# First head of the expert routing: where its query weights lie, shift products ahead of the query, squares summed on VectorE, and eight choices routed first

## The chip, the cores and the metric

The kernel runs on one core of one Trainium2 chip. The metric is device time in microseconds (us) of one execution; the time before is the median of three runs. The engines are TensorE (PE in the rows; PEld is its weight load), VectorE (DVE), ScalarE (ACT), GpSimd (POOL) and SyncE (SP). SP issues the weight loads in one queue, POOL issues the gathers in its own, and ACT issues a few small loads.

## The reference, cut to what matters

Two transformer blocks on 256 tokens of width 1024. The first block ends with `peer`, a layer of 16,384 tiny experts that the tokens choose by product keys:

```python
qh = (t @ w_q).reshape(T, PEER_HEADS, 2, PEER_KEY_DIM // 2)
s = jnp.einsum('thpd,hpnd->thpn', qh, sub_keys)      # 128 keys in each of 2 halves
s_top, i_top = lax.top_k(s, PEER_TOPK)               # 16 of each half
cand = s_top[:, :, 0, :, None] + s_top[:, :, 1, None, :]
cand_idx = i_top[:, :, 0, :, None] * PEER_N_KEYS + i_top[:, :, 1, None, :]
best, pos = lax.top_k(cand.reshape(T, PEER_HEADS, 256), PEER_TOPK)
idx = jnp.take_along_axis(cand_idx..., pos, axis=-1)
g = jax.nn.softmax(best, axis=-1)
ue, ve = jnp.take(u_tab, idx, axis=0), jnp.take(v_tab, idx, axis=0)
act = jax.nn.gelu(jnp.einsum('thkd,td->thk', ue, t))
return jnp.einsum('thk,thkd->td', g * act, ve)
```

There are 8 heads, and `t` is the normed and shifted input: x times a gain, divided by its root mean square, plus a shift from the modulation. Each token sums 8 times 16 experts, one row of `u_tab` and one of `v_tab` for each.

## The kernel before, in words

The 256 tokens are two tiles of 128. A head and a tile make a step s = 2 * head + tile, so there are 16 steps of 16 choices. For each choice POOL gathers one row of the joined table `uv` (1024 floats of u and 1024 of v) for each of 128 tokens: 256 gathers of 1 MB. They land in a ring of NR = 13 places (tag `uv`). For each, `first` takes the dot product of the u half with the token's row `ht` on VectorE (L943) and the Gelu on ScalarE (L944); `second` makes a diagonal tile `dgw` on VectorE (L952) and multiplies it with the v half in 8 products on TensorE. When `second` is done the place is free and the next gather is issued. The steps of `routing(s + 2)` stand between the dots of step s.

What stands ahead of the first gather: the last products of the previous stage (the `wmix` sum, weights split into high and low parts `whi`, `wlo`, `wlox`), the sum into `x` (L408), then head 0's query (`query_early`). `project` multiplies head 0's query weights `wq` with `xg`, which is x times the gain but not yet normed; so the scores are scaled afterwards by `rs` (from the sums of squares, L351 and L353), and the part that the shift contributes (`pc`, then `pb`: products of the modulation columns with `wq`, and of the result with the keys `ks`) is added. `routing(0)` follows on VectorE: the best 8 of each half (L812, L813), the next 8 (L814 to L816), the 256 sums `cd`, their best 16, and `decode`, which turns positions into row numbers `IX` with one-hot tiles `oh` (L915 to L922). Only then are `normed` and `rows` issued (the normed input `hf`, and its transposed rows `ht`), and gathers go out.

The weights of the eight query heads are loaded by SP in one queue: heads 0 to 3 into four places of the ring, 1 MB each, heads 4 to 7 in halves into places of the earlier weight tiles (`raw`, `whi`, `wlo`). The first nine gathers take ring places that hold no weights, the tenth takes head 0's, and the eleventh to the thirteenth need those of heads 1, 2 and 3, which their projections free. In the program as built, head 0's place is one whose former content was last read by an early product of the `wmix` sum. The place of `ht` lies at bytes 217,888 to 226,080 of each partition, over the last two low parts of `wmix` (bytes 215,808 to 224,000).

Of the kernel before, what the change touches and what calls it, by code (L numbers as in the profile page):

```python
# [113 lines left out]
class Kern:  # L114
# [641 lines left out]
    def phase_b(self):  # L756
# [4 lines left out]
        with ExitStack() as es:  # L761
# [10 lines left out]
            def qload(h):  # L772

                if h < 4:
                    g = rows_.tile([P, 2 * D], F32, name="wq", tag="uv", bufs=NR)
                    self.take(g[:].rearrange("p (u c) -> p u c", u=2), A["wpq"][2 * h:2 * h + 2].rearrange("u p c -> p u c"))
                    wq[h] = [g[:, 0:D], g[:, D:2 * D]]
                else:
                    wq[h] = []
                    for u in (2 * h, 2 * h + 1):  # L780
                        g = self.slot("r", ["raw", "whi", "raw", "whi", "raw", "whi", "wlo", "wlo"][u - 8], F32, "st")
                        self.take(g[:], A["wpq"][u])
                        wq[h].append(g[:])

            self.inturn = True
            for h in range(8):
                qload(h)
# [11 lines left out]
            ht = rows_.tile([P, 2, D], F32, name="ht")  # L799

            def rows():

                for t in range(2):
                    for h in range(2):
                        ps = self.rot("tr")
                        for k in range(4):
                            nc.tensor.transpose(ps[:, k * 128:k * 128 + 128], hf[:, 4 * h + k, t * 128:t * 128 + 128], self.con("ident"))
                        nc.scalar.activation(ht[:, t, h * 512:h * 512 + 512], ps[:], AF.Copy)

            def top16(v, idx, s, n):  # L810
                s2 = wk.tile([P, n], F32, name="s2", tag=f"s2{n}", bufs=1)
                nc.vector.max(v[:, 0:8], s)  # L812
                nc.vector.max_index(idx[:, 0:8], v[:, 0:8], s)  # L813
                nc.vector.match_replace(s2[:], v[:, 0:8], s, -3e38)  # L814
                nc.vector.max(v[:, 8:16], s2[:])
                nc.vector.max_index(idx[:, 8:16], v[:, 8:16], s2[:])  # L816
# [11 lines left out]
            def keys(h, ps):  # L828

                ks = wk.tile([P, 256], F32, name="ks", tag="ks", bufs=2)  # L830
                nc.gpsimd.dma_start(ks[:], A["keysT"][h]) if h < 2 else nc.scalar.dma_start(ks[:], A["keysT"][h])
# [15 lines left out]
            def query_early():  # L847

                ps = project(0, xg)
                sums = self.square_sums(x)  # L850
                rs = self.rms_col(sums)
                sc, ks, end = keys(0, ps)

                pc = self.rot("mm")
                with self.tc.issue_after(end):
                    for a in range(2):
                        for k in range(KT):
                            self.mm(pc[:, a * 128:a * 128 + 128], wq[0][a][:, k * 128:k * 128 + 128],
                                    self.mod[:, 24 + k:25 + k].to_broadcast([P, 128]), k == 0 and a == 0, k == KT - 1 and a == 1)
                cb = wk.tile([P, 256], F32, name="cb", tag="s2256", bufs=1)  # L860
                nc.scalar.activation(cb[:], pc[:, 0:256], AF.Copy)
                pb = self.rot("mm")
                for a in range(2):
                    self.mm(pb[:, a * 128:a * 128 + 128], cb[:, a * 128:a * 128 + 128], ks[:, a * 128:a * 128 + 128])
                for t in range(2):
                    c = slice(t * 256, t * 256 + 256)
                    nc.scalar.activation(scores[0][:, c], sc[:, c], AF.Copy, scale=rs[:, t:t + 1])
                ss = scores[0][:].rearrange("p (t k) -> p t k", t=2)
                nc.vector.tensor_tensor(ss, pb[:, 0:256].unsqueeze(1).to_broadcast([P, 2, 256]), ss, OP.add)
                return rs  # L870

            def normed(rs):
                self.spread(rs, bc[:])
# [5 lines left out]
            IX, WT = {}, {}  # L879

            def routing(s):
# [6 lines left out]

                def half(a):
                    ss = scores[h]  # L890
                    top16(SV[:, a, :], SI[:, a, :], ss[:, t * 256 + a * 128:t * 256 + a * 128 + 128], 128)
# [13 lines left out]
                def decode():  # L905
                    si = wk.tile([P, 2, 16], F32, name="si", tag="si", bufs=1)
                    nc.vector.tensor_scalar(si[:, 0, :], SI[:, 0, :], 128.0, None, op0=OP.mult)
                    nc.vector.tensor_copy(si[:, 1, :], SI[:, 1, :])
                    ab = wk.tile([P, 2, 16], U32, name="ab", tag="ab", bufs=1)
                    nc.vector.tensor_scalar(ab[:, 0, :], BI[:], 4, None, op0=OP.logical_shift_right)  # L910
                    nc.vector.tensor_scalar(ab[:, 1, :], BI[:], 15, None, op0=OP.bitwise_and)
                    af = wk.tile([P, 2, 16], F32, name="af", tag="af", bufs=1)
                    nc.vector.tensor_copy(af[:], ab[:])
                    oh = wk.tile([P, 2, 16, 16], F32, name="oh", tag="oh", bufs=1)
                    nc.vector.tensor_tensor(oh[:].rearrange("p a k c -> p (a k) c"),  # L915
                                            self.con("iota", 16).unsqueeze(1).to_broadcast([P, 32, 16]),
                                            af[:].rearrange("p a k -> p (a k)").unsqueeze(2).to_broadcast([P, 32, 16]), OP.is_equal)
                    nc.vector.tensor_tensor(oh[:], oh[:], si[:].unsqueeze(2).to_broadcast([P, 2, 16, 16]), OP.mult)
                    ix = wk.tile([P, 2, 16], F32, name="ixf", tag="ixf", bufs=1)
                    nc.vector.tensor_reduce(ix[:], oh[:], mybir.AxisListType.X, OP.add)  # L920
                    IX[s] = wk.tile([P, 16], U32, name="IX", tag="IX", bufs=4)
                    last = nc.vector.tensor_tensor(IX[s][:], ix[:, 0, :], ix[:, 1, :], OP.add).ins  # L922
# [5 lines left out]
                return [lambda: half(0), lambda: half(1), pairs, decode]  # L928
# [4 lines left out]
            def fetch(s, k):  # L933
                g = ring[s, k] = rows_.tile([P, 2 * D], F32, name="uv", tag="uv", bufs=NR)
                nc.gpsimd.indirect_dma_start(out=g[:], out_offset=None, in_=A["uv"],  # L935
                                             in_offset=bass.IndirectOffsetOnAxis(ap=IX[s][:, k:k + 1], axis=0))

            def first(s, k):
# [4 lines left out]
                dot = nc.vector.tensor_tensor_reduce(u, u, ht[:, t, :], 1.0, 0.0, OP.mult, OP.add, accum_out=a[:, 0:1]).ins  # L943
# [16 lines left out]
            rs = query_early()  # L960
            for step in routing(0):
                last = step()
            with self.tc.issue_after(last):
                normed(rs)
                rows()
                for step in routing(1):
                    step()
            choices = [(s, k) for s in range(16) for k in range(16)]
# [534 lines left out]
```

## Time and profile before

| what | value |
|---|---|
| three runs | 1529.53, 1532.02, 1536.04 us |
| the profiled execution's own time | 1538.33 us |
| its span | 1536.2 us |
| mean granted TensorE clock | 0.987 |
| busy: PE, PEld, DVE, ACT, POOL | 91%, 83%, 76%, 39%, 23% |
| chain that ended last | PE 49%, DMA 30%, DVE 14%, issue 4% |
| moved by DMA | 433.40 MB, of it 269.24 MB by POOL's gathers |

The profiled execution took 6.3 us more than the median of the three runs. Shares over the whole span mix three parts: a stretch up to about 265 us in which TensorE works through dense products, the gathers from 265 to about 920 us, and the second block from there on. In rows with two numbers in front, the first is the start in us from the span's start and the second the time in us.

### The profile page before, as it was taken

Reading aid. Unit: us, or ns where it says so; the run is one execution under the profiler, and the core shown is the slowest. Engines: PE = TensorE matmul, PEld = TensorE weight load, DVE = VectorE, ACT = ScalarE, POOL = GpSimd, SP = SyncE. Lnnn points to the kernel's source line nnn. Section 1 sums busy time; section 2 is a strip of 40 time slices with the busy share of each in tenths; the row PEclk is TensorE's granted clock in tenths of the full one; section 3 lists DMA queues with packets and bytes.
Section 4 is the critical chain, followed back from the end, with each engine's and each line's share of the span. In section 5 each row is a group of like instructions: output and inputs, shape, how many; then the busy total and the mean of one; then the engine's idle time right before and its main releaser. Section 6 shows DMA issues by size and latency. Waiting matters only on the chain.

```text
span 1536.2 us, 28266 instructions
## 1 busy us (share of the span) xinstructions
PE 1391.3 (91%) x10732; PEld 1275.5 (83%) x10732; DVE 1171.4 (76%) x2760; ACT 603.5 (39%) x1227; POOL 353.0 (23%) x316
## 2 busy tenths in 40 slices
PE   8999986999998787888688889999999999999998
PEld 2898886898987777777677779989999996899997
DVE  4898764897897779776566557976988888588885
ACT  2646532411211113111110004775655568555553
POOL 0000000343465555555455530000000000000000
PEclk9999998999999999999999999999999999999999
DMA  9667745999999999999999994434655542355550
GB/s 349 231 233 264 236 169 212 383 401 421 370 425 426 426 426 426 426 426 426 425 426 426 426 416 163 137 125 151 206 187 185 190 154 97 111 193 188 184 190 28
DMA packets 82839, 433.40 MB, mean 282 GB/s; under 512 B 9296, under 2 KB 10448, under 8 KB 49680
## 3 DMA queue, kind: packets, MB, share of 16 engines
q0 software_dynamic: 37120, 269.24, 42.1%
q1 hardware_dynamic: 43712, 159.67, 30.5%
q10 hardware_dynamic: 1872, 2.68, 0.5%
q8 instruction: 85, 1.39, 0.4%
q14 instruction: 50, 0.41, 0.1%
HBM read 430.51 MB, written 1.05 MB: 281 GB/s over the span
## 4 chain that ended last, share of the span: by engine, by line
PE 49%; DMA 30%; DVE 14%; issue 4%; ACT 1%; POOL 0%; another core or an unknown queue 0%; DVEq 0%; POOLq 0%; SPq 0%; ACTq 0%
PE b L132 48%; DMA uv<-in_uv,IX 27%; DVE uv L943 2%; DMA rawx<-in_wmodT 1%; DVE wlo L209 1%; DVE wlox L209 1%; DVE dgw L952 1%; DVE rawx L488 1%; DMA raw<-in_wmodT 1%; DVE raw L488 1%; DVE s L814 1%; DMA raw<-in_wqkv 1%; DVE SI L816 0%; DVE oh L915 0%; DVE SI L813 0%
## 5 line engine op out<-in xcount | busy, mean ns | idle before, releaser
L132 PE MATMUL b<-dgw,uv 128*128 128x128 f32 x4096 | 506.0, 279 | 99.2 <-DVE dgw L952 98.6
L132 PEld LDWEIGHTS b<-dgw,uv 128*128 128x128 f32 x4096 | 473.0, 192 | 133.4 <-DVE dgw L952 131.8
L943 DVE CUSTOM_DVE_ANT_0 uv<-uv,ht 128x1024 f32<-128x1024 f32 x256 | 312.4, 1220 | 143.6 <-DMA uv<-in_uv,IX 142.0
L935 POOL DMA_INDIRECT uv<-in_uv,IX x256 | 330.3, 1290 | 331.7 <-DMA uv<-in_uv,IX 138.4
L132 PE MATMUL b<-H,whi 128*128 128x256 f32 x1296 | 245.0, 287 | 3.6 <-DVE mx L1041 1.4
L944 ACT ACTIVATE act<-act 128x1 f32<-128x1 f32 x256 | 51.3, 202 | 499.3 <-DVE act L943 489.7
L132 PE MATMUL b<-H,wlox 128*128 128x256 f32 x824 | 231.7, 281 | 0.0
L132 PE MATMUL b<-H,whix 128*128 128x256 f32 x1216 | 221.5, 282 | 0.0
L132 PEld LDWEIGHTS b<-H,whi 128*128 128x128 f32 x1296 | 201.4, 189 | 10.6 <-issue 5.0
L132 PEld LDWEIGHTS b<-H,whix 128*128 128x128 f32 x1216 | 186.7, 188 | 5.3 <-issue 3.0
L132 PEld LDWEIGHTS b<-H,wlox 128*128 128x128 f32 x824 | 155.6, 189 | 0.4 <-issue 0.3
L132 PE MATMUL b<-H,wlo 128*128 128x256 f32 x440 | 122.3, 288 | 0.0
L952 DVE TENSOR_SCALAR dgw<-cn,act,we 128x128 f32<-128x128 f32 x256 | 87.6, 342 | 14.3 <-ACT act L944 14.2
L209 DVE TENSOR_TENSOR wlox<-rawx,whix 128x1024 fp32r<-128x1024 f32 x60 | 73.1, 1222 | 31.7 <-ACT whix L200 30.9
L200 ACT ACTIVATE whix<-rawx 128x1024 fp32r<-128x1024 f32 x60 | 63.0, 1058 | 74.8 <-PE b L132 63.1
L200 ACT ACTIVATE whi<-rawx 128x1024 fp32r<-128x1024 f32 x59 | 62.2, 1058 | 60.1 <-PE b L132 60.1
L209 DVE TENSOR_TENSOR wlox<-raw,whix 128x1024 fp32r<-128x1024 f32 x57 | 69.6, 1221 | 19.0 <-ACT whix L200 18.4
L200 ACT ACTIVATE whi<-raw 128x1024 fp32r<-128x1024 f32 x58 | 61.0, 1056 | 56.9 <-PE b L132 45.8
L132 PEld LDWEIGHTS b<-H,wlo 128*128 128x128 f32 x440 | 82.2, 188 | 1.2 <-issue 0.7
L200 ACT ACTIVATE whix<-raw 128x1024 fp32r<-128x1024 f32 x57 | 60.3, 1058 | 54.0 <-PE b L132 50.8
L353 POOL TENSOR_TENSOR rs<-ms,nhalf 128x2 f32<-128x2 f32 x6 | 6.2, 1027 | 312.9 <-DVE ms L351 312.9
L1256 DVE SCALAR_TENSOR_TENSOR c<-u,cl,c 128x256 f32<-128x256 f32 x176 | 73.7, 478 | 0.8 <-ACT c L1253 0.7
(348 smaller groups left out, 2240.8 us busy)
## 6 DMA issues: line engine op xcount, KB each, us to landing
rawx<-in_wup SPq DMA_DIRECT2D x45, 512.0 KB, 3.3
raw<-in_wup SPq DMA_DIRECT2D x43, 512.0 KB, 3.3
raw<-in_wdn SPq DMA_DIRECT2D x23, 512.0 KB, 3.2
rawx<-in_win SPq DMA_DIRECT2D x21, 512.0 KB, 4.6
rawx<-in_wdn SPq DMA_DIRECT2D x21, 512.0 KB, 3.3
rawx<-in_wmodT SPq DMA_DIRECT2D x18, 512.0 KB, 4.1
raw<-in_wmodT SPq DMA_DIRECT2D x14, 512.0 KB, 3.4
raw<-in_win SPq DMA_DIRECT2D x13, 512.0 KB, 5.1
```

The lines of the kernel that those rows point to most:

```text
L132: return self.nc.tensor.matmul(out, lhsT, rhs, start=start, stop=stop).ins
L200: nc.scalar.activation(hi[:], raw[:], AF.Copy)
L209: nc.vector.tensor_sub(u.lo[:], u.raw[:], u.hi[:].bitcast(F32))
L353: nc.gpsimd.tensor_tensor(rs[:], ms[:], self.nhalf[:, 0:2], OP.pow)
L488: self.nc.vector.tensor_tensor_reduce(r, r, row[h][:], 1.0, self.mod[:, at:at + 1] if h else self.col("bmod", at), OP.mult, OP.add, accum_ ...
L814: nc.vector.match_replace(s2[:], v[:, 0:8], s, -3e38)
L935: nc.gpsimd.indirect_dma_start(out=g[:], out_offset=None, in_=A["uv"], in_offset=bass.IndirectOffsetOnAxis(ap=IX[s][:, k:k + 1], axis=0))
L943: dot = nc.vector.tensor_tensor_reduce(u, u, ht[:, t, :], 1.0, 0.0, OP.mult, OP.add, accum_out=a[:, 0:1]).ins
L944: nc.scalar.activation(a[:, 1:2], a[:, 0:1], AF.Gelu)
L952: done = nc.vector.tensor_scalar(dg[:], self.con("ident"), a[:, 1:2], e[:, k:k + 1], op0=OP.mult, op1=OP.mult).ins
L1256: nc.vector.scalar_tensor_tensor(c[:, a, :], u[:, a, j:j + 256], self.col("cw2", at + 44 * j), c[:, a, :], op0=OP.mult, op1=OP.add)
```

## The change

- Head 0's weights are given the place of `ht` (tag `ht`, one buffer) in place of a ring place; heads 1 and 2 lie in ring places, heads 3 to 6 in places of earlier weight tiles, and head 7 is loaded later, at choice 36, into head 3's places. So seven heads are loaded ahead of the gathers where there were eight, and three projections ahead of the first dot become two (`query` of heads 3 to 7 stands at choices 8, 36, 68, 100, 132, where heads 4 to 7 stood at 8, 36, 68, 100).
- The shift products `pc` stand ahead of `project(0)`; the squares of x are added on VectorE (3 adds of 128x512), which leaves 4 column-sum products where there were 16.
- The scores of head 0 are one operation for each tile on VectorE (scores * rs + shift part), where ScalarE scaled and VectorE added.
- `first8` routes 8 choices from the best 8 of each half (64 sums) into `IX8`; the first 8 gathers use it, and only then do the normed input, the rows and the rest of `routing(0)` follow. Gathers 9 to 13 use `IX`, which holds all 16.
- The prefetch of `wqkv` stands at choice 136 (was 104), and `angles` at 144 (was 120).

SP's queue, where the query weights begin (before with -, after with +; `wq` are whole heads, `raw`, `whi` and `wlo` halves; in brackets the semaphores waited for):

```order
 L181 DMA raw<-in_wmix 128x1024 [waits DMAHW7_49,DVE_49]
-L181 DMA wq<-in_wpq 128x2x1024 [waits PE_49]
-L181 DMA wq<-in_wpq 128x2x1024 [waits DVE_49,DMAHW0_49,PE_49,Activation_49]
-L181 DMA wq<-in_wpq 128x2x1024 [waits DMAHW5_49,DMAHW3_49]
-L181 DMA wq<-in_wpq 128x2x1024 [waits DMAHW4_49]
-L181 DMA raw<-in_wpq 128x1024
+L181 DMA wq<-in_wpq 128x2x1024 [waits DVE_49,PE_49]
+L181 DMA wq<-in_wpq 128x2x1024 [waits DMAHW3_49]
+L181 DMA wq<-in_wpq 128x2x1024 [waits DMAHW4_49,DMAHW0_49,Activation_49]
+L181 DMA raw<-in_wpq 128x1024 [waits DMAHW5_49]
```

The first whole head waited for PE alone, and now waits for PE and DVE: in the program as built, the PE count that it waits for is the one that the last `wmix` product raises, because that product reads the low part which lies where head 0's weights now go. Heads 1 and 2 stand behind it in the same queue.

TensorE, from the last `wmix` product to head 0's scores and the spread of `rs`, before:

```order
L132 MATMUL b_2146<-mh,wlox 128x256
L132 MATMUL b_2623<-cn_69,sq 128x1 x4
L132 MATMUL b_2606<-H_2556,wq 128x256 x16
L132 MATMUL b_2623<-cn_69,sq 128x1 x12
L132 MATMUL b_2656<-ks,qT 128x128 x4
L132 MATMUL b_2662<-mod,wq 128x128 x16
L132 MATMUL b_2681<-ks,cb 128x128 x2
L132 MATMUL b_2734<-dg,cn_69 128x256
```

The same place after:

```order
L132 MATMUL b_2146<-mh,wlox 128x256
L132 MATMUL b_2603<-mod,wq 128x128 x16
L132 MATMUL b_2632<-H_2556,wq 128x256 x16
L132 MATMUL b_2649<-cn_69,sq 128x1 x4
L132 MATMUL b_2660<-ks,cb 128x128 x2
L132 MATMUL b_2665<-ks,qT 128x128 x4
L132 MATMUL b_2676<-dg,cn_69 128x256
```

The shift products (`mod,wq`) moved from behind the scores to the front, and 12 of 16 column sums are gone.

VectorE, from the best 8 of head 0's 64 sums on, after (`cd_2689` holds the sums, `IX_2693` is `IX8`, `t_` are tiles of the normed input):

```order
L820 MAX best<-cd_2689 128x8
L821 MAX_INDEX BI<-best,cd_2689 128x8
L928 TENSOR_SCALAR ab<-BI 128x8
L929 TENSOR_SCALAR ab<-BI 128x8
L931 CAST af<-ab 128x16
L933 TENSOR_TENSOR oh<-cn_69,af 128x128
L936 TENSOR_TENSOR oh<-oh,si 128x128
L938 TENSOR_REDUCE ixf<-oh 128x16
L939 TENSOR_TENSOR IX_2693<-ixf 128x8
L903 TENSOR_TENSOR t_2724<-H_2556,bc_72 128x256
L903 TENSOR_TENSOR t_2727<-H_2556,bc_72 128x256
L827 MATCH_REPLACE s_2773<-SV,ss 128x128
```

The decode of the first eight row numbers, 128 elements wide, follows one round on 64 candidates, and the second rounds (`MATCH_REPLACE`) come behind it; before, two rounds for each half, two on 256 candidates and a decode 512 elements wide stood ahead of any row number.

The diff, cut to its core:

```diff
-                if h < 4:
-                    g = rows_.tile([P, 2 * D], F32, name="wq", tag="uv", bufs=NR)
+                if h < 3:
+                    g = rows_.tile([P, 2 * D], F32, name="wq", tag="uv" if h else "ht", bufs=NR if h else 1)
+                    wq[h] = [g[:, 0:D], g[:, D:2 * D]]
+                    return g
+                wq[h] = [self.slot("r", w, F32, "st") for w in
+                         ("wlo" if h == 6 else "raw", "wlo" if h == 6 else "whi")]
...
+            places = {h: qplace(h) for h in (2, 1, 0)}
             self.inturn = True
-            for h in range(8):
-                qload(h)
+            for h in range(7):
+                if h >= 3:
+                    qplace(h)
+                qload(h, places.get(h))
             self.inturn = False
...
-                ps = project(0, xg)
-                sums = self.square_sums(x)
-                rs = self.rms_col(sums)
-                sc, ks, end = keys(0, ps)
 
                 pc = self.rot("mm")
...
+                sq = [wk.tile([P, 512], F32, name="sq", tag=t, bufs=n) for t, n in [("oh", 1), ("qT", 2), ("qT", 2)]]
+                for b in range(4):
+                    q = sq[b] if b < 2 else sq[2]
+                    nc.scalar.activation(q[:], x[:, 2 * b:2 * b + 2, :].rearrange("p a t -> p (a t)"), AF.Square)
+                    if b:
+                        nc.vector.tensor_tensor(sq[0][:], sq[0][:], q[:], OP.add)
+                with self.tc.issue_after(end):
+                    ps = project(0, xg)
...
+                    nc.vector.scalar_tensor_tensor(scores[0][:, c], sc[:, c], rs[:, t:t + 1], sb[:], op0=OP.mult, op1=OP.add)
                 return rs
...
+                def first8():
+
+                    for a in range(2):
+                        top8(SV[:, a, :], SI[:, a, :], of(a))
+                    cd = wk.tile([P, 64], F32, name="cd8", tag="s2128", bufs=1)
+                    nc.vector.tensor_tensor(cd[:].rearrange("p (a b) -> p a b", a=8),
+                                            SV[:, 0, 0:8].unsqueeze(2).to_broadcast([P, 8, 8]),
+                                            SV[:, 1, 0:8].unsqueeze(1).to_broadcast([P, 8, 8]), OP.add)
+                    top8(best, BI, cd[:])
+                    early.append(wk.tile([P, 8], U32, name="IX8"))
+                    return parts(8, 8, BI[:, 0:8], 3, early[0][:])
...
-            for c in choices[0:NR]:
-                fetch(*c)
-            for h in range(1, 4):
+            choices = [(s, k) for s in range(16) for k in range(16)]
+            query_early()
+            steps = routing(0)
+            last = steps.pop(0)()
+            for c in choices[0:8]:
+                fetch(*c)
+            with self.tc.issue_after(last):
+                normed()
                 rows()
+                for step in steps:
+                    last = step()
+            for c in choices[8:NR]:
+                fetch(*c)
+            with self.tc.issue_after(last):
                 for step in routing(1):
                     step()
...
+            for h in range(1, 3):
                 query(h)
...
-                if n in (8, 36, 68, 100):
-                    query(4 + n // 32)
-                if n == 104:
+                if n in (8, 36, 68, 100, 132):
+                    query(3 + n // 32)
+                if n == 36:
+                    qplace(7)
+                    qload(7)
+                if n == 136:
                     self.allowed = "ac"
                     self.fetch([])
-                if n == 120:
+                if n == 144:
```

## Rows read from the trace of the kernel before

**Rows 1.** The page, DMA rate (GB/s) in 40 equal slices of the span (38.4 us each)

```profile
GB/s 349 231 233 264 236 169 212 383 401 421 370 425 426 426 426 426 426 426 426 425 426 426 426 416 163 137 125 151 206 187 185 190 154 97 111 193 188 184 190 28
```

**Rows 2.** Timeline of POOL: start us, time us, operation, idle before and its releaser

```profile
264.98 1.06 POOL L935 DMA_INDIRECT uv<-in_uv,IX  x1 [16.67 <-DVE SV L812]
...
280.31 0.94 POOL L935 DMA_INDIRECT uv<-in_uv,IX  x1 [2.81 <-PE b L132]
289.38 0.94 POOL L935 DMA_INDIRECT uv<-in_uv,IX  x1 [8.13 <-PE b L132]
297.27 1.61 POOL L935 DMA_INDIRECT uv<-in_uv,IX  x1 [6.95 <-PE b L132]
...
909.02 1.38 POOL L935 DMA_INDIRECT uv<-in_uv,IX  x1 [1.06 <-DMA uv<-in_uv,IX]
```

**Rows 3.** Windows: busy us of each engine, granted clock, DMA share, GB/s

```profile
257.00:265.00 8.00, 0.38 (x1) 0.41 (x2) 7.70 (x34) 0.40 (x2) 0.02 (x1) 0.60 0.00 0
290.00:340.00 50.00, 47.65 (x367) 45.72 (x367) 50.00 (x195) 15.54 (x33) 19.27 (x19) 1.00 0.95 376
...
380.00:420.00 40.00, 39.25 (x316) 38.08 (x315) 32.27 (x85) 9.55 (x26) 18.70 (x16) 1.00 0.98 369
450.00:900.00 450.00, 361.74 (x2883) 333.11 (x2881) 317.64 (x776) 67.17 (x219) 239.00 (x179) 1.00 1.01 426
```

**Rows 4.** Timeline of SP, the queue of the weight loads

```profile
216.79 0.43 SPq L181 DMA_DIRECT2D wq<-in_wpq  x1
...
237.02 2.52 SPq L181 DMA_DIRECT2D wq<-in_wpq  x3
...
242.04 0.33 SPq L181 DMA_DIRECT2D raw<-in_wpq  x1
```

**Rows 5.** Timeline of PE, from the last wmix product to head 0's shift part

```profile
236.66 0.28 PE L132 MATMUL b<-mh,wlox 128*128 128x256 f32 x1
...
236.78 0.95 PE L132 MATMUL b<-cn,sq 128*128 128x1 f32 x8
...
237.59 7.15 PE L132 MATMUL b<-H,wq 128*128 128x256 f32 x32
...
247.18 1.14 PE L132 MATMUL b<-ks,qT 128*128 128x128 f32 x8
...
248.15 5.37 PE L132 MATMUL b<-mod,wq 128*128 128x128 f32 x32
...
253.99 0.71 PE L132 MATMUL b<-ks,cb 128*128 128x128 f32 x4 [0.47 <-ACT cb L861]
```

**Rows 6.** Windows around two falls of the clock (columns as in Rows 3)

```profile
248.00:252.00 4.00, 4.00 (x23) 4.00 (x23) 0.00 (x0) 0.84 (x2) 0.31 (x1) 0.57 1.03 421
...
258.00:260.00 2.00, 0.00 (x0) 0.00 (x0) 1.93 (x10) 0.00 (x0) 0.00 (x0) 0.67 0.00 0
260.00:272.00 12.00, 5.55 (x15) 3.89 (x16) 11.72 (x50) 5.01 (x12) 5.50 (x6) 0.50 0.43 156
```

**Rows 7.** Timeline of DVE and POOL, from the sum into x to the first row numbers

```profile
236.98 0.88 DVE L408 SCALAR_TENSOR_TENSOR x<-b,g1h,x 128x256 f32<-128x256 f32 x2 [0.55 <-PE b L132]
...
247.35 0.16 DVE L351 TENSOR_SCALAR ms<-b 128x2 f32<-128x2 f32 x1 [9.49 <-PE b L132]
247.60 0.72 POOL L353 TENSOR_TENSOR rs<-ms,nhalf 128x2 f32<-128x2 f32 x1 [19.15 <-DVE ms L351]
...
255.53 0.49 DVE L812 MAX8 SV<-ss 128x8 f32<-128x128 f32 x2
...
256.00 0.28 DVE L813 FIND_INDEX8 SI<-SV,ss 128x8 uint32<-128x128 f32 x1
...
258.42 0.40 DVE L895 TENSOR_TENSOR cd<-SV 128x256 f32<-128x256 f32 x1
...
261.74 0.69 DVE L915 TENSOR_TENSOR oh<-cn,af 128x512 f32<-128x512 f32 x1
...
263.91 0.17 DVE L922 TENSOR_TENSOR IX<-ixf 128x16 uint32<-128x16 f32 x1
```

More of the change, by code (lines that the diff above doesn't have):

```diff
@@ L770, in phase_b, with qplace, qload @@
             wq = {}
[L772 to L783 removed]
+            def qplace(h):
+                if h < 3:
[4 more added lines that the diff above has]
+                         ("wlo" if h == 6 else "raw", "wlo" if h == 6 else "whi")]
+            def qload(h, g=None):
+                if g is not None:
+                    self.take(g[:].rearrange("p (u c) -> p u c", u=2), A["wpq"][2 * h:2 * h + 2].rearrange("u p c -> p u c"))
+                    return
+                for u in range(2):
+                    self.take(wq[h][u][:], A["wpq"][2 * h + u])
+            places = {h: qplace(h) for h in (2, 1, 0)}
             self.inturn = True
[L786 to L787 removed]
+            for h in range(7):
+                if h >= 3:
+                    qplace(h)
+                qload(h, places.get(h))
             self.inturn = False
@@ L847, in query_early @@
             def query_early():
-                ps = project(0, xg)
-                sums = self.square_sums(x)
-                rs = self.rms_col(sums)
-                sc, ks, end = keys(0, ps)
                 pc = self.rot("mm")
[L855 to L859, printed above, removed]
+                for a in range(2):
+                    for k in range(KT):
+                        end = self.mm(pc[:, a * 128:a * 128 + 128], wq[0][a][:, k * 128:k * 128 + 128],
+                                      self.mod[:, 24 + k:25 + k].to_broadcast([P, 128]), k == 0 and a == 0, k == KT - 1 and a == 1)
                 cb = wk.tile([P, 256], F32, name="cb", tag="s2256", bufs=1)
                 nc.scalar.activation(cb[:], pc[:, 0:256], AF.Copy)
+                sq = [wk.tile([P, 512], F32, name="sq", tag=t, bufs=n) for t, n in [("oh", 1), ("qT", 2), ("qT", 2)]]
[6 more added lines that the diff above has]
+                    ps = project(0, xg)
+                sums = self.rot("tr")
+                for h in range(2):
+                    for t in range(2):
+                        self.mm(sums[:, t:t + 1], sq[0][:, h * 256 + t * 128:h * 256 + t * 128 + 128], self.con("ones", 1),
+                                h == 0 and t == 0, h == 1 and t == 1)
+                rs = self.rms_col(sums)
+                ks = wk.tile([P, 256], F32, name="ks", tag="ks", bufs=2)
+                nc.gpsimd.dma_start(ks[:], A["keysT"][0])
                 pb = self.rot("mm")
@@ new lines, in first8 @@
+                def first8():
+                    for a in range(2):
+                        top8(SV[:, a, :], SI[:, a, :], of(a))
[6 more added lines that the diff above has]
+                    return parts(8, 8, BI[:, 0:8], 3, early[0][:])
@@ L926, in decode @@
                     return last
-                return [lambda: half(0), lambda: half(1), pairs, decode]
+                return [first8] * (s == 0) + [lambda: half(0), lambda: half(1), pairs, decode]
             big = self.bigs()
@@ L935, in fetch @@
                 nc.gpsimd.indirect_dma_start(out=g[:], out_offset=None, in_=A["uv"],
-                                             in_offset=bass.IndirectOffsetOnAxis(ap=IX[s][:, k:k + 1], axis=0))
+                                             in_offset=bass.IndirectOffsetOnAxis(
+                                                 ap=early[0][:, k:k + 1] if s == 0 and k < 8 else IX[s][:, k:k + 1], axis=0))
             def first(s, k):
```

77 lines of the change are left out of this document (40 added, 37 removed).

## The prediction

> **What bounds the kernel now.** I began with the page's DMA rates by slice [rows 1]: from the twelfth slice to the twenty-third (422 to 883 us) the rate is flat at 425 or 426 GB/s. There the kernel is bound by its transfers, in the middle of a span whose busiest engine is TensorE. Next the queue of POOL [rows 2]: the first gather is issued at 264.98 us and the 256th at 909.02, so 255 pitches take 644.04 us, 2.53 us each. At 426 GB/s a gather of 1.0486 MB takes 2.46 us. The stretch is thus nearly all transfer, and behind it stands the second block, which starts with its result. The end of the kernel moves with two things: when the first gather goes out, and how much DMA time is lost after that.
>
> The windows show where it is lost [rows 3]. From 257 to 265 us nothing moves at all while VectorE is busy for 7.70 of 8 us: this is the routing, for which the first gather waits. From 290 to 340 the rate is 376 GB/s, a loss of (426 - 376)/426 x 50 = 5.9 us, with VectorE busy for all 50 us. From 380 to 420 it is 369, a loss of 5.4 us, with PE busy for 39.25 of 40 us. From 450 to 900 nothing is lost.
>
> Then the road to the first gather. PE ends the last wmix product at 236.94 us, runs head 0's projection at 237.59 (7.15 us), the scores at 247.18, the shift products at 248.15 (5.37 us) and their product with the keys at 253.99 [rows 5]. VectorE adds the scores and starts the routing at 255.53, has the last row number at 264.08, and POOL issues 0.90 us later [rows 7, 2]. Head 0's weights do not hold this up: they are issued at 216.79, and PE doesn't wait for them [rows 4, 5].
>
> **The change part by part.**
>
> *Weights of head 0.* The load now waits for the count of the last wmix product, since it is written over the low part which that product reads. The row for such a load is the next one of before: heads 1 to 3 are issued at 237.02, behind the same product, and SP's issue that waits for head 1's transfer comes at 242.04 [rows 4]. So I take head 0's weights at 242.04, 5.0 us after their issue; the bounds are 2.5 us (the bytes alone at 426 GB/s) and 7.5 (one more such transfer ahead of them). They land late, not early, and PE has nothing else to do: it idles from 236.94 to 242.04, 5.1 us.
>
> *Shift products first.* They take 5.37 us in before, at a granted clock of 0.57 in 248 to 252 [rows 5, 6]. All at full clock they would take half of the projection's 7.15 (half as many columns), 3.6; all at half clock 7.2. After 5.1 idle us a fall is to be expected: PE's idling from 254.7 brought the clock to 0.67 in 258 to 260 and 0.50 then [rows 6]. I take the row, 5.4, since PE works here without gaps as it did there; bounds 3.6 and 7.2. They end at 247.4.
>
> [...]
>
> *Projection, sums, scores.* Projection 7.15 us [rows 5]: 254.6. The four sums that remain are eight records, 0.95 us as the first eight were: 255.5. Behind them PE runs the keys' products, 0.71 and 1.14 [rows 5]: 257.3. Beside that VectorE and POOL make rs, from 247.35 to 248.32 in before, 0.97 us [rows 7], and the spread's two tiles: hidden. The scores are now two VectorE operations of the form of the sum into x, 0.88 us [rows 7]: 258.2. The squares and their three adds of 128x512 (0.69 us each by the oh row [rows 7], 2.1 together) are hidden, as they lie in the wait for weights and under the projection; uncovered they would cost 2.1.
>
> *First 8 choices.* The routing of before takes 8.55 us: 2.89 to the sums, 3.32 to the one-hot tiles, 2.34 from there [rows 7]. Of the first part one round of two stays: 0.49 for MAX8 and two FIND_INDEX8 of 0.28, 1.05. Of the second: sums, MAX8 and FIND_INDEX8 over 64 candidates, each at most the 128-wide 0.28, and five small conversions near the 0.17 of IX: 1.6. Of the third, three operations of 128 elements in place of 512, between 0.17 and 0.28, and IX: 0.9. Sum 3.5 (bounds 2.8 and 4.5). IX8 stands at 261.7, the first gather goes at 262.6 with the same 0.90. Against 264.98 that is **-2.4 us**. By the bounds of landing (-2.5, +2.5), clock (-1.8, +1.8) and routing (-0.7, +1.0) it lies between -7.4 and +2.9.
>
> *The next fetches.* The first eight gathers keep the queue for 8 x 2.46 = 19.7 us, to about 284. The ninth waits for the full row numbers; VectorE still has some 5 us of routing and the normed input's products to do, so it comes at about 275, 9 us ahead of need. That cover gone, each us of lateness costs one.
>
> *Places and queries.* The eleventh to thirteenth gather wait in before for heads 1, 2 and 3, until 297.27 [rows 2]. Now heads 1 and 2 alone hold places, and the first second products stand behind two queries, not three. A query is 7.15 + 1.14 = 8.3 us of PE. At each point up to 420 us PE has done one query less. In 290 to 340 this helps little, since VectorE is the full engine there [rows 3], and gets some 2 us more to do (the 64 sums, their round and a second decode). In 380 to 420 PE is the full one. So of 5.9 + 5.4 us lost I take **-3** back, a bit over half of the second; bounds 0 and -11.3.
>
> *Head 7.* Its 1 MB goes in after head 3's projection, among the gathers: **+2.5 us** [rows 3], nothing if it falls where the rate is below 426. I keep the full price. The wqkv prefetch and the angles move within the stretch, where PE has 88 us free of 450 [rows 3], and are needed behind it: nothing. Uncovered, the wqkv halves would cost their transfer, 1.2 us each.
>
> *Sum.* -2.4 - 3 + 2.5 = **-2.9 us**. The profiled execution's own time is 1538.3, so this would be 1535.4; it stands 6.3 above the median of the three runs, 1532.0, and against that the time is **1529**.
>
> **The rivals.** What a measurement of this kernel can tell from no change is about 0.5%, 7.7 us.
>
> *Weights that do land early.* If the wait is on an earlier product after all, PE goes from the last wmix product into the shift products at full clock: 5.1 us of idling and 1.8 of clock go, start -9.3, with the rest -9.8, time 1522. For it: the place of before needed no such wait [rows 4]. Against it: the place itself, and what the wait counts.
>
> *The lost DMA time comes back.* If PE's missing query refills the ring from 290 on, the 11.3 us come back: -2.4 - 11.3 + 2.5 = -11.2, 1521; three quarters give -8.4. For it: PE is busy for 47.65 of 50 us too in 290 to 340. Against it: VectorE's 50 of 50 [rows 3].
>
> *The clock stays down* (slower). The clock was 0.50 from 260 to 272 though PE had begun to work again at 264 [rows 6]. If it holds through the shift products and the projection, they take 7.2 + 14.3 in place of 5.4 + 7.15: +8.9. The start is then 6.5 later than before, and the whole +6.0, 1538; without the 3 us taken back, +9, 1541. It decides from 2.9 us of surcharge, where the gain is gone. Against it: in 260 to 272 PE was busy for 5.55 of 12 us alone; here it works without gaps.
>
> **How the numbers follow.** The forecast (late weights, -6 to +2) 0.56, early weights 0.09, the lost time back 0.15, clock down 0.13, something else 0.07. Faster by over 0.5%: most of the second and of the third, 0.21, and 0.03 of the rest: 0.24. Slower by over 0.5%: a third of the fourth and half of the unknown: 0.08. The same: 0.68. The range leaves out little beyond the ends of the rivals: 1521 to 1538, about eight in ten.
>
> **What would show it.** Right: wq's first issue at 237.0 and PE idle to about 242; a granted clock near 0.5 there; first gather at 262 to 263; thirteenth gather before 290; a rate above 376 in the 50 us from 288. Wrong: shift products at 237 to 238; a projection of over 10 us; a first gather behind 265; a ninth behind 284; a rate below 369 around 400 us.

## The result: slower, and the profile after

The changed kernel takes 1547.12 us (median of 4 runs, 1545.05 to 1548.28) where the kernel before takes 1532.87 (median of 4, 1529.53 to 1536.04): a ratio of 1.0089, 95% interval 1.0070 to 1.0108. That is 14 us slower. The forecast was 1529 and its range ended at 1538.

The page's DMA rates come first again, in 40 slices of 38.6 us:

```profile
GB/s 339 238 232 273 231 135 249 419 417 404 375 419 419 419 419 419 419 419 418 418 419 419 419 407 162 133 128 151 204 190 181 190 150 96 109 186 185 189 190 29
```

Against [rows 1] the hole in the seventh and eighth slice is smaller (249 and 419 where 212 and 383 stood), so the gathers do begin earlier. But the plateau is at 419 GB/s (418 in two slices) and not at 426, in the eighth slice already and from the twelfth to the twenty-third. That is 1.6% less over the 650 us that bind the kernel.

The stretch ahead of the gathers went as forecast. SP issues the three whole heads behind the last wmix product; columns as in [rows 4]:

```profile
237.52 1.41 SPq L181 DMA_DIRECT2D wq<-in_wpq  x3
```

PE waits 4.97 us for them, and then runs the shift products, the projection, the four sums and the scores [rows 5]:

```profile
242.46 5.43 PE L132 MATMUL b<-mod,wq 128*128 128x128 f32 x32 [4.97 <-DMA wq<-in_wpq]
247.74 7.07 PE L132 MATMUL b<-H,wq 128*128 128x256 f32 x32
254.64 0.95 PE L132 MATMUL b<-cn,sq 128*128 128x1 f32 x8
...
255.98 1.06 PE L132 MATMUL b<-ks,qT 128*128 128x128 f32 x8
```

The granted clock of the same time (columns as in [rows 3]) is 0.63 and then 0.51 when the shift products start after the wait. It is full, 1.00, from 246 us on, in the last 1.9 us of the shift products and at the start of the projection:

```profile
242.00:244.00 2.00, 1.54 (x7) 1.57 (x8) 0.38 (x1) 0.00 (x0) 0.00 (x0) 0.63 1.02 418
244.00:246.00 2.00, 2.00 (x12) 2.00 (x11) 0.00 (x0) 0.00 (x0) 0.00 (x0) 0.51 1.02 414
246.00:248.00 2.00, 2.00 (x19) 1.98 (x19) 0.00 (x0) 0.07 (x1) 0.00 (x0) 1.00 1.03 403
```

VectorE adds the squares in the wait (239.50), forms the scores at 257.14 and routes eight choices from 257.94 to 261.34, 3.40 us, where the routing of before took 8.55 [rows 7]:

```profile
239.50 1.49 DVE L877 TENSOR_TENSOR sq<-sq 128x512 f32<-128x512 f32 x2 [1.10 <-ACT sq L875]
...
257.14 0.88 DVE L897 SCALAR_TENSOR_TENSOR ss<-b,rs,sb 128x256 f32<-128x256 f32 x2
257.94 0.48 DVE L820 MAX8 SV<-ss 128x8 f32<-128x128 f32 x2
...
261.17 0.17 DVE L939 TENSOR_TENSOR IX<-ixf 128x8 uint32<-128x8 f32 x1
```

The first gather goes at 262.19 (264.98 in [rows 2]), the ninth at 274.67 with its row numbers, the thirteenth at 281.54 (297.27 before). But the last one goes at 915.89, where it went at 909.02:

```profile
262.19 1.06 POOL L980 DMA_INDIRECT uv<-in_uv,IX  x1 [5.60 <-DVE t L903]
...
274.67 0.94 POOL L980 DMA_INDIRECT uv<-in_uv,IX  x1 [1.13 <-DVE SV L820]
...
281.54 0.94 POOL L980 DMA_INDIRECT uv<-in_uv,IX  x1 [1.36 <-PE b L132]
...
915.89 1.39 POOL L980 DMA_INDIRECT uv<-in_uv,IX  x1 [2.08 <-PE b L132]
```

The windows say the same. Where before had 376 GB/s from 290 to 340 us [rows 3] there are 418; but where before had 426, from 450 to 900, there are 419:

```profile
290.00:340.00 50.00, 46.57 (x341) 42.80 (x340) 49.98 (x198) 13.19 (x29) 22.13 (x18) 1.00 1.01 418
340.00:380.00 40.00, 36.92 (x258) 33.16 (x257) 30.19 (x102) 6.86 (x19) 16.85 (x12) 1.00 1.01 408
380.00:420.00 40.00, 40.00 (x334) 39.20 (x333) 38.61 (x115) 11.23 (x31) 20.07 (x18) 1.00 0.99 374
...
450.00:900.00 450.00, 354.96 (x2803) 325.69 (x2802) 310.91 (x758) 65.10 (x213) 232.24 (x176) 1.00 1.01 419
```

Two rows of the kernel before belong beside these. The first is its window from 340 to 380 us; the second is its window from 290 to 340 in a second profile of the unchanged kernel (e0 below):

```profile
340.00:380.00 40.00, 37.56 (x271) 34.40 (x270) 30.39 (x103) 6.12 (x19) 16.73 (x14) 1.00 1.01 426
```

```profile
290.00:340.00 50.00, 47.90 (x371) 45.97 (x370) 50.00 (x196) 15.43 (x33) 18.88 (x19) 1.00 0.99 398
```

So of the 42 GB/s between 376 and 418, 22 are no more than two profiles of one kernel differ by; and from 340 to 380 us the kernel before moves 426 where the changed one has 408.

To compare runs of several chips I cut each profile at five events: the start of the last wmix product, the issue of the first and of the last gather, the first operation on x behind the experts (933.01 us in before, 939.25 after), and the end of the span. The table holds all profiles of this study; "ring" is the first byte of the ring in a partition, as built, less the multiple of 256 below it.

| kernel | ring | wmix starts at | to first gather | to last gather | to x | to the end |
|---|---|---|---|---|---|---|
| before | 0 | 236.66 | 28.32 | 644.04 | 23.99 | 603.19 |
| before again (e0) | 0 | 238.68 | 28.33 | 641.43 | 23.97 | 600.19 |
| before, shifted (e2) | 32 | 236.16 | 28.32 | 652.86 | 24.39 | 606.47 |
| after | 32 | 237.21 | 24.98 | 653.70 | 23.36 | 606.45 |
| after again (e5) | 32 | 241.14 | 25.01 | 653.29 | 23.37 | 601.49 |
| after, 64 bytes (e3) | 64 | 238.54 | 24.78 | 650.96 | 23.29 | 603.53 |
| after, 128 bytes (e6) | 128 | 237.36 | 26.43 | 651.48 | 23.22 | 603.61 |
| after, 256 bytes (e1) | 0 | 235.89 | 24.74 | 643.62 | 22.90 | 603.25 |
| e1 without head 7's load (e9) | 0 | 239.30 | 25.39 | 643.46 | 22.92 | 601.93 |
| e1 with three queries first (e10) | 0 | 240.28 | 25.44 | 642.18 | 22.90 | 604.90 |
| after without the early eight (e7) | 0 | 235.71 | 30.02 | 642.80 | 23.90 | 600.47 |
| e1 with early weights (e4) | 0 | 237.34 | 18.23 | 644.53 | 22.91 | 606.19 |
| e4 with later queries (e8) | 0 | 240.24 | 18.24 | 642.49 | 23.88 | 603.35 |
| e4 with eight heads first (e11) | 0 | 236.74 | 18.20 | 642.95 | 23.87 | 606.24 |

Between the first two profiled executions of before and after, 9.5 us of span differ: +0.55 ahead of wmix, -3.34 to the first gather, +9.66 among the gathers, -0.63 behind them, +3.26 in the second block. The second block's length goes from 600.2 to 606.5 over all kernels without regard to the change, so these 3 us are not its doing.

### The profile page after: what moved, and what is told of

The parts are those of the page before. It is cut to its first block, busy times and chain, and to the rows that moved or that the text cites. A ratio compares the mean times of both kernels' runs of the same rounds, so it can differ in the third digit from the quotient of the medians.

```text
span 1545.7 us, 28242 instructions
## 1 busy us (share of the span) xinstructions
PE 1395.7 (90%) x10708; PEld 1276.2 (83%) x10708; DVE 1174.7 (76%) x2777; ACT 604.9 (39%) x1228; POOL 357.7 (23%) x315
## 4 chain that ended last, share of the span: by engine, by line
PE 48%; DMA 32%; DVE 14%; issue 5%; ACT 1%; POOL 0%; DVEq 0%; POOLq 0%; SPq 0%; ACTq 0%
PE b L132 47%; DMA uv<-in_uv,IX 29%; DVE uv L989 2%; DMA rawx<-in_wmodT 1%; DVE wlox L209 1%; DVE wlo L209 1%; DVE dgw L998 1%; DVE s L827 1%; DMA raw<-in_wmodT 1%; DMA raw<-in_wqkv 1%; DVE rawx L488 1%; DVE raw L488 0%; DVE oh L936 0%; DVE SI L821 0%; PE b L1104 0%
## 5 line engine op out<-in xcount | busy, mean ns | idle before, releaser
L980 POOL DMA_INDIRECT uv<-in_uv,IX x256 | 335.8, 1312 | 324.9 <-DMA uv<-in_uv,IX 159.1
L132 PE MATMUL b<-H,whi 128*128 128x256 f32 x1312 | 250.6, 289 | 3.3 <-DVE mx L1095 1.4
L132 PEld LDWEIGHTS b<-H,whi 128*128 128x128 f32 x1312 | 205.0, 189 | 10.4 <-issue 5.0
L209 DVE TENSOR_TENSOR wlox<-rawx,whix 128x1024 fp32r<-128x1024 f32 x60 | 73.1, 1223 | 32.7 <-ACT whix L200 31.9
```

The lines of the kernel that those rows point to most:

```text
L132: return self.nc.tensor.matmul(out, lhsT, rhs, start=start, stop=stop).ins
L209: nc.vector.tensor_sub(u.lo[:], u.raw[:], u.hi[:].bitcast(F32))
```

## The experiments

**The place of the ring.** The theory, formed after the result: the change adds one tile of 8 row numbers, `IX8`, 32 bytes in each partition, and the tiles allocated behind it move up by 32 bytes, `dgw`, the ring and `ht` among them. The ring's places started at 111,360 = 435 x 256 before and start at 111,392 after. (The bytes given above for the place of `ht`, 217,888, are those of the changed program; in the one before it lay at 217,856. The difference stood there to be read.) If a gather into a place off a multiple of 256 is slower, that is the 10 us. The rivals: head 7's load or the new order slows the gathers (L), or the two profiles differ by chance (R).

Padding the new tile alone (e1):

```diff
-                    early.append(wk.tile([P, 8], U32, name="IX8"))
-                    return parts(8, 8, BI[:, 0:8], 3, early[0][:])
+                    early.append(wk.tile([P, 64], U32, name="IX8"))
+                    return parts(8, 8, BI[:, 0:8], 3, early[0][:, 0:8])
```

> The changed kernel with IX8 64 columns wide (256 bytes) in place of 8 (32 bytes): nothing is computed otherwise, but the 13 ring places start at multiples of 256 bytes again (111,616 in place of 111,392). Theory P (the place of the ring slows the gathers): the rate from 450 to 900 us is 426 GB/s as in the kernel before, not 419; a pitch of 2.46 us and not 2.50, so the last gather is issued some 10 us earlier, near 906, and the time is 1536 (1533 to 1539). Rival L (head 7's load, the 8 early gathers or something else of the new order slows them): 419 GB/s and 1547 as the changed kernel. Rival R (the two profiles differ by chance): any rate.

The window from 450 to 900 us and the first and last gather of e1:

```profile
450.00:900.00 450.00, 360.12 (x2862) 330.99 (x2861) 314.43 (x758) 65.93 (x217) 239.70 (x179) 1.00 1.01 426
```

```profile
260.63 1.06 POOL L980 DMA_INDIRECT uv<-in_uv,IX  x1 [5.60 <-DVE t L903]
...
904.25 1.38 POOL L980 DMA_INDIRECT uv<-in_uv,IX  x1 [2.03 <-PE b L132]
```

The rate is 426 again, the stretch 643.62 us. Time 1535.15 (7 runs), 0.9965 of before on that chip, interval 0.9950 to 0.9979. So the change as it was meant is faster, by 0.35%, and its new tile's 32 bytes turn that into a loss. That the time lies in the expected 1533 to 1539 is luck: the 1536 was meant beside the 1533 of the first chip, 3 us slower than before, and on this chip before takes 1540.89.

The counterpart is the kernel before with 32 bytes more (e2):

```diff
-            a2 = wk.tile([P, 8], F32, name="a2")
-            nc.vector.scalar_tensor_tensor(a2[:], self.mod[:, 32:40], 1.0, self.col("n2", 0, 8), op0=OP.add, op1=OP.mult)
+            a2 = wk.tile([P, 16], F32, name="a2")
+            nc.vector.scalar_tensor_tensor(a2[:, 0:8], self.mod[:, 32:40], 1.0, self.col("n2", 0, 8), op0=OP.add, op1=OP.mult)
```

> The kernel before, with one small tile (a2) 16 columns wide in place of 8, the upper 8 unused: the same instructions, but the ring starts at 111,392 bytes as in the changed kernel, 32 bytes off a multiple of 256. Theory P: 419 GB/s from 450 to 900 us, the last gather some 10 us later, near 919, and 1543 us (1540 to 1546) where the kernel before has 1533. Rivals L and R: 426 GB/s, last gather near 909, 1533.

```profile
450.00:900.00 450.00, 355.75 (x2831) 327.20 (x2831) 313.27 (x765) 67.59 (x217) 231.71 (x177) 1.00 1.01 419
```

```profile
264.48 1.06 POOL L935 DMA_INDIRECT uv<-in_uv,IX  x1 [16.67 <-DVE SV L812]
...
917.34 1.38 POOL L935 DMA_INDIRECT uv<-in_uv,IX  x1 [1.12 <-DMA uv<-in_uv,IX]
```

It has the same instructions as the kernel before, and its road to the first gather is the same 28.32 us; the rate falls to 419 and the stretch grows from 644.04 to 652.86. Time 1552.34, 1.0075 of before, interval 1.0058 to 1.0092. The 1543 expected were again counted from the first chip's 1533; the difference is 11.5 us where 10 were expected. L is out, since nothing of the change but the place is in this kernel. R is out by all profiles of the table together: the rate from 450 to 900 us is 426 in each of the nine with the ring at a multiple of 256, and 419 or 420 in each of the five others.

One rival more has to be answered, since `dgw` and `ht` moved with the ring: that VectorE or TensorE work slower on them. From 450 to 900 us a dot takes 1223 ns in the kernel before and 1224 in the changed one, a `dgw` 343 and 344 ns and a second product 280 and 281 ns, and the DMA share is 1.01 in both, at 426 and 419 GB/s. So the transfers themselves take longer, and the gathers write nowhere but into the ring.

How far the place must be off, with `IX8` at 64 bytes (e3, below) and at 128 (e6, with 32 in place of 16):

```diff
-                    early.append(wk.tile([P, 8], U32, name="IX8"))
-                    return parts(8, 8, BI[:, 0:8], 3, early[0][:])
+                    early.append(wk.tile([P, 16], U32, name="IX8"))
+                    return parts(8, 8, BI[:, 0:8], 3, early[0][:, 0:8])
```

> The changed kernel with IX8 16 columns wide (64 bytes): the ring starts at 111,424, a multiple of 64 but not of 128 or 256. [...] Theory P in the form of 64-byte steps: 426 GB/s, 1536. Rival L: 419 and 1547 whatever the place.

> The changed kernel with IX8 32 columns wide (128 bytes): the ring starts at 111,488, a multiple of 128 but not of 256. If only multiples of 256 are quick: 419 to 420 GB/s as at 32 and 64 bytes, last gather near 914. If multiples of 128 do: 426, last gather near 905.

```profile
450.00:900.00 450.00, 355.27 (x2819) 326.04 (x2818) 312.39 (x763) 65.91 (x216) 234.55 (x176) 1.00 1.01 420
```

```profile
450.00:900.00 450.00, 355.00 (x2816) 325.79 (x2815) 312.66 (x766) 66.16 (x215) 234.30 (x177) 1.00 1.01 420
```

The first row is e3, the second e6: 420 both, and stretches of 650.96 and 651.48. A multiple of 128 is not enough. 32 bytes off took about 2 us more than 64 or 128 (652.86 to 653.70), which is inside the scatter found below. Of the time there is one run each, 1543.04 and 1543.95, from which no verdict follows.

The changed kernel once more (e5, no edit):

> The changed kernel itself, again, beside the next runs: by the place of the ring it has to come out 1.2% above the padded kernel and 0.7 to 1.1% above the kernel before, 419 GB/s from 450 to 900 us. If the 0.89% of the first comparison was a chance of its chip, it comes out within 0.5% of before, still at 419.

```profile
450.00:900.00 450.00, 355.94 (x2803) 326.95 (x2803) 311.60 (x764) 67.56 (x217) 233.28 (x175) 0.99 1.01 419
```

The rate and the stretch repeat, 419 GB/s and 653.29 us against 653.70. The time doesn't: 1546.79 against 1541.99 of before, 1.0031, interval 1.0012 to 1.0049. The expected 0.7 to 1.1% was missed, and by the expectation's own words part of the first 0.89% was a chance of its chip. This chip's runs of before spread over 10 us (1537.56 to 1547.58). The sign holds on both chips; the interval of the first, 1.0070 to 1.0108, doesn't meet this one, and with no profile of before from this chip it stays open which part differs. By the table, from wmix to the first operation on x, the changed kernel is 5.3 to 8.3 us slower (its two profiles against the two of before), so the 4.8 us of this chip are nearer to what the stages show than the 14 of the first.

And the kernel before once more (e0, no edit):

> The kernel before, unchanged, profiled again, to see which parts of its time repeat. From the last wmix product to the first gather 28.3 us and from there to the last gather 644.0 us should repeat within 1 us, since two kernels of one ring place and one order gave that so far (the changed kernel 653.7 and 653.3). If the stretch came out near 653 here, the 10 us would be a chance of the run and not the place's. What differs between chips is expected ahead of the last wmix product (235.9 to 241.1 in the runs so far) and behind the experts (600.5 to 606.5).

28.33 us repeats, but the stretch came out 2.6 us shorter than in the first profile, where I had expected 1. The 2.6 us lie in the window from 290 to 340 us, 398 GB/s for 376: (398 - 376)/426 x 50 = 2.6. So a single profile resolves the stretch to some 3 us. The nine profiles with the ring at multiples of 256 lie between 641.43 and 644.53, the five others between 650.96 and 653.70.

**Early weights.** In e4 the heads 0 to 2 all lie in the ring, head 0 in the place that is free early; the padding of e1 is kept:

```diff
-                    g = rows_.tile([P, 2 * D], F32, name="wq", tag="uv" if h else "ht", bufs=NR if h else 1)
+                    g = rows_.tile([P, 2 * D], F32, name="wq", tag="uv", bufs=NR)
...
-            places = {h: qplace(h) for h in (2, 1, 0)}
+            places = {h: qplace(h) for h in (0, 2, 1)}
```

> The padded changed kernel (ring at multiples of 256 bytes) with heads 0, 1 and 2 all in ring places, head 0 in the one that is free early, so that its weights are issued near 217 us and not behind the last wmix product at 237. By the forecast's steps: no idling of PE from 237 to 242, shift products at full clock (3.6 us), first gather near 256 (it was at 262.2 in the changed kernel), 6 us or so below the padded kernel at the end, 1530. Rival: the lead is lost again to VectorE and the ring before 450 us, and the time is that of the padded kernel within 2 us.

SP's first issue and PE's shift products and projection in e4:

```profile
217.45 21.93 SPq L181 DMA_DIRECT2D wq<-in_wpq  x3
```

```profile
237.46 3.73 PE L132 MATMUL b<-mod,wq 128*128 128x128 f32 x32
241.03 7.07 PE L132 MATMUL b<-H,wq 128*128 128x256 f32 x32
```

The weights are issued at 217.45, and the shift products follow the last wmix product at full clock (1.00 from 238 to 242 us), 3.73 us (5.43 in the changed kernel, 5.19 in e1, where the clock is 0.66 from 240 to 242 us and 0.50 from 242 to 244). From wmix to the first gather it takes 18.23 us and not 24.74: 6.5 us, of which 5.0 are the wait and 1.5 the clock. The stretch keeps its length, 644.53 for 643.62, and 5.6 of the 6.5 us are left at the first operation on x. Time 1531.11, 0.9924 of before, interval 0.9903 to 0.9946, which doesn't meet e1's 0.9950 to 0.9979 on the same chip; the medians differ by 4.0 us where 6 were expected. The rival (the lead is lost before 450 us) is out.

**The early eight choices.** e7 is the changed kernel with the whole routing ahead of all gathers, in the order of before, and without `IX8`:

```diff
-                return [first8] * (s == 0) + [lambda: half(0), lambda: half(1), pairs, decode]
+                return [lambda: half(0), lambda: half(1), pairs, decode]
...
-            last = steps.pop(0)()
-            for c in choices[0:8]:
+            for step in steps:
+                last = step()
+            for c in choices[0:NR]:
                 fetch(*c)
```

> The changed kernel without the early eight choices: the whole routing of step 0, then all gathers, and no IX8, so the ring lies at 111,360, a multiple of 256. All else stays. The early choices save 8.55 - 3.5 = 5 us ahead of the first gather by the forecast's routing term, so the first gather is expected near 266 to 267 (padded kernel 260.6), the last x operation 5 us later than the padded kernel's, 0.9992 of before. Rival: VectorE is full up to 350 us and does less in all without a second decode, so half of the 5 us come back before 450 and the end is only 2 us later.

```profile
265.73 1.06 POOL L980 DMA_INDIRECT uv<-in_uv,IX  x1 [10.75 <-DVE t L903]
```

30.02 us to the first gather, 5.3 more than e1, so the early choices are worth what was reckoned (8.55 - 3.5 = 5.05). 30.02 is also 1.7 us more than before. If late weights cost the 6.5 us of e4, the new order of products and sums saves 4.8 of them; no run has that order alone. Time 0.9996 of before where 0.9992 was expected, interval 0.9976 to 1.0016. By the stages, in single profiles, 4.5 us of the 5.3 are left at the last gather and 5.5 at the first operation on x, so the rival (2 us) is not borne out.

**Queries and head 7.** e9 lets head 7's query use head 6's weights, and e10 goes back to three queries ahead of the first dot:

```diff
-                    qplace(7)
-                    qload(7)
+                    wq[7] = wq[6]
```

> The padded changed kernel (ring at multiples of 256 bytes) without head 7's load: head 7's query uses head 6's weights, so its 16 choices in each of the two last steps are not the reference's. It shows what that 1 MB among the gathers costs. From the first to the last gather the padded kernel took 643.6 us. The forecast's term says 2.5 less, 641.1. Rival: the load falls at 305 to 340 us, where VectorE sets the pace and the ring has a lead, and the pace from there hides it: 643 to 644.

```diff
-            for h in range(1, 3):
+            for h in range(1, 4):
                 query(h)
...
-                if n in (8, 36, 68, 100, 132):
-                    query(3 + n // 32)
+                if n in (8, 36, 68, 100):
+                    query(4 + n // 32)
```

> The padded changed kernel with three queries ahead of the first dot, as in the kernel before (heads 4 to 7 at choices 8, 36, 68, 100), and all else of the change. It shows whether the query that is missing on PE gives the lost DMA time back. By the forecast's step (PE has one query less up to 420 us) the 3 us come off again: 646 to 647 from the first to the last gather, in place of 643.6. Rival: only the ring places count, and the pace is VectorE's: 643 to 644.

Neither moves the stretch: 643.46 and 642.18, with 643.62 in e1. For e9 the expected 2.5 us are no more than two profiles of one kernel differ by, so one profile speaks against the term without settling it. For e10 the expected +3 came out as -1.4. The rate from 290 to 340 us is 424 GB/s in e10 and 425 in e1, so it doesn't hang on the missing query. Of the time there is one run each (1534.76 and 1537.77), and no verdict.

e8 is e4 with later queries (head 7's load at 72, the prefetch at 172, the angles at 180):

```diff
-                if n in (8, 36, 68, 100, 132):
-                    query(3 + n // 32)
+                if n in (40, 72, 104, 136, 168):
+                    query(2 + n // 32)
```

> The kernel with early weights (head 0's load at 217 us, ring at multiples of 256), with the queries of heads 3 to 7 at choices 40, 72, 104, 136, 168 in place of 8, 36, 68, 100, 132, head 7's load at 72, the prefetch at 172 and the angles at 180. PE is full from 380 to 420 us and the rate falls to 371 to 393 there and in 340 to 380, 8 us lost in all; a query is 8.3 us of PE, and one more leaves that stretch. If PE's queries are what empties the ring: the rate stays above 410 in both windows and the end comes 4 to 7 us earlier, 1525 on this chip. If VectorE is: no change within 2 us.

The windows from 340 to 380 and 380 to 420 us, e8 first and then e10:

```profile
340.00:380.00 40.00, 37.25 (x266) 33.76 (x265) 30.19 (x103) 9.81 (x24) 16.84 (x12) 1.00 1.00 390
380.00:420.00 40.00, 39.38 (x329) 38.44 (x328) 38.60 (x117) 8.63 (x26) 21.18 (x19) 1.00 0.98 383
```

```profile
340.00:380.00 40.00, 38.52 (x268) 34.68 (x268) 32.52 (x119) 4.88 (x17) 18.62 (x13) 1.00 1.01 424
380.00:420.00 40.00, 40.00 (x333) 39.08 (x332) 38.61 (x113) 12.04 (x32) 20.31 (x18) 1.00 0.96 373
```

Taking queries off PE in e8 does not fill the two windows (390 and 383 GB/s; e4 had 393 and 371), and its stretch of 642.49 is 2 us below e4's, which is inside the scatter. PE is busy for 37.25 and 39.38 of 40 us in them. Which chain between VectorE's dots and PE's second products empties the ring there stays open. Time of e8: 1529.43, 0.9921 of before, interval 0.9898 to 0.9945, the same as e4.

e11 keeps the new order of the products, the early eight and the padding, with the loads and queries of the kernel before:

```diff
-                if h < 3:
+                if h < 4:
...
-            for h in range(7):
-                if h >= 3:
-                    qplace(h)
-                qload(h, places.get(h))
+            for h in range(8):
+                qload(h)
```

> The best of both: the shift products first, squares on VectorE, eight choices early, the ring at multiples of 256 bytes, and the loads and queries of the kernel before (heads 0 to 3 in ring places, head 0 early, heads 4 to 7 behind them, three queries ahead of the first dot). First gather some 18 us after the last wmix product, as with early weights (before 28.3); from the first to the last gather 644 if head 7's 2.5 us and the lost relief of 3 us cancel; time 0.992 of before, as with early weights and seven heads. If the relief is PE's, it is 0.5 us worse; if head 7's load is what counts, up to 2.5 better.

18.20 us, 642.95 us, time 1531.09, 0.9944 of before, interval 0.9925 to 0.9963. So moving head 7 and a query is worth nothing that can be told: the versions e4, e8 and e11 beat the kernel before by 0.6 to 0.8%. All three have weights that are there in time, the new order of products, early choices, and a ring at a multiple of 256 bytes. Their first gather goes out 18.2 us after the wmix product where it took 28.3.

## Why the prediction was wrong

The step that failed is one that the text took as fixed: "At 426 GB/s a gather of 1.0486 MB takes 2.46 us." It was read from before and carried over to the changed kernel, since no instruction of a gather changes. The tile IX8 was reckoned as VectorE work alone, and that it moves what lies behind it was not asked. At 419 GB/s a gather takes 2.50 us, and 256 x 0.041 = 10.5 us; the stretch grew by 9.7 us between the two profiles, and by 8.8 in the kernel before with nothing but the shift. No rival held this, so the range couldn't either. Nor did the signs: every one named for being right came true (418 GB/s in the 50 us from 288, for the rate), and none for being wrong, but none of them asked for the rate after 420 us.

The other steps, one by one:

- *Weights of head 0* (late, at hand 5.0 us after their issue at 237, PE idle to 242): right. Issue 237.52, idling 4.97 us. The rival with weights that land early is out for this kernel; e4 shows what it would have brought: the start moved by 6.5 us against the 6.9 reckoned (5.1 + 1.8).
- *Shift products* at 5.4 us, bounds 3.6 and 7.2: 5.43, at a granted clock of 0.63 and 0.51 and full before the projection. That the row fits to 0.03 us is luck: after the same wait of 5.0 to 5.1 us they took 5.19 in e1 and 6.74 in e6, and those 1.55 us are most of the 1.69 by which e6's 26.43 us to its first gather exceed e1's 24.74. The clock rival (clock down in the projection too) is out: the projection took 7.07, at 1.00 from 248 to 254 us. The clock was 0.51 in 244 to 246 us, after 4.97 us of waiting, and 1.00 in e4, where PE did not wait. That the wait alone sets it is not shown: in before it was 0.57 from 248 to 252 us with PE busy for all 4 us [rows 6]. The price was 5.43 - 3.73 = 1.7 us against e4, where 1.8 had been taken; in e1 it was 1.5 and in e6 3.0.
- *First 8 choices*, 3.5 us: 3.40. First gather 262.19 where 262.6 was forecast: -2.8 by the span's clock and -3.3 counted from the last wmix product, for -2.4.
- *The next fetches*: the ninth gather at 274.67 for "about 275", with no gap behind it (419 GB/s from 275 to 280 us). The "about 284" beside it is 282.3 by its own terms, 262.6 + 19.7; nothing hangs on it.
- *Places and queries* (-3) and *head 7* (+2.5): their sum, -0.5, matches e1's stretch (-0.4 against the first profile of before, +2.2 against e0), but by chance: taken one by one in e10 and e9 neither showed. The 42 GB/s more from 290 to 340 us [rows 3], half of them scatter, were partly lost again from 340 to 380, where 408 stand in the row of after and 426 in that of before.
- The *sum* of these terms, -2.9 us, with +10.5 for the place, is +7.6; the profiles differ by 9.5, of which 3.3 lie in the second block, and the medians by 14. What makes up the rest of the 14 is not shown. e1, where the place is right, came out at 0.9965: -5.4 us on that chip's 1540.89.

That the cause is the place is shown, in both directions. Why a place 32, 64 or 128 bytes off a multiple of 256 costs 1.4 to 1.7% is not shown by these runs.

## What to carry to other kernels

When a kernel is bound by gathers into a ring, the first byte of the ring belongs to what is read of a change: compare it in both programs as built, and pad a new small tile that lies ahead of it to a multiple of 256 bytes (here `IX8` at 256 bytes left 426 GB/s, and at 32, 64 and 128 it left 419 to 420). A rate that was flat over hundreds of us is worth a look in the profile after before anything else, because 1.6% of it outweighs a stall of 3 us that the change removes. And terms that cancel in a sum are not confirmed by the sum.

## What the runs showed of the hardware that I had not expected

The place of a gather's rows in a partition changes its rate: 426 GB/s in the nine profiles with the ring at a multiple of 256 bytes, 419 at 32 bytes off (three profiles), 420 at 64 and at 128 off. From 500 to 700 us POOL issues 79 gathers in the changed kernel and 81 in the padded one (the number behind the count is not used here):

```profile
uv<-in_uv,IX POOLq DMA_INDIRECT x79, 19.2
```

```profile
uv<-in_uv,IX POOLq DMA_INDIRECT x81
```
